# A two-layer diffusion block on Trainium2: modulation rows share the ring of raw weights

## The chip, the core and the metric

The kernel runs on one core of a Trainium2 chip. The core has TensorE (PE, with its weight loads as PEld), VectorE (DVE), ScalarE (ACT), GpSimd (POOL), and SyncE (SP), which here only issues DMAs. Each engine works through its own instructions in order; semaphores hold an instruction back until its inputs are there. The metric is the device time of one execution in microseconds (us), as a median of several.

## The reference

Two transformer layers work on 512 tokens `x` and 256 tokens of context, with a width of 1024, all in float32. A layer is a feed forward, an attention (grouped queries with a window in layer 0, differential in layer 1) and a second feed forward. Each is preceded by a norm with shift and gain and scaled by a gate. These nine vectors per layer are the modulation: one product of a condition with a 1024 x 9216 matrix, for the tokens and for the context.

```python
for i in range(DEPTH):
    mx = (silu_c @ ada_w[i] + ada_b[i]).reshape(B, N_MOD, 1, D)
    mc = (silu_cc @ ada_w[i] + ada_b[i]).reshape(N_MOD, D)
    fx = _swiglu(_pre(hx, norm_w[i, 0], mx[:, 0], mx[:, 1]), ffn_w_gate[i, 0], ...)
    hx = hx + 0.5 * mx[:, 2] * fx        # the same for hc with mc
    ...                                  # attention with mx[:, 3..5]
    ...                                  # second feed forward with mx[:, 6..8]
return _rmsnorm(hx, final_norm_w)
```

`_swiglu` is `(silu(h @ gate) * (h @ up)) @ down` with an inner width of 2816. In the last layer only `x` is needed behind the attention.

## The kernel before

**Tiling.** Tokens lie along the free axis (768 of them), features on the 128 partitions in 8 blocks. A float32 product is made of parts: each operand is split into a high part in the matmul's format and a low part (the rest), and three matmuls are added up: high by high, high by low, low by high.

**Weights.** `weights()` brings one unit: a DMA of 512 KB from SP into `w_raw` (L54), ACT's cast to `w_hi` (L55) and POOL's subtraction to `w_lo` (L56). All three names have two buffers each, so a unit's cast must wait until PE has finished the unit two before it. A unit of a projection serves 48 matmuls (L265).

**A feed forward** (`ffn`, run four times: in the trace from 0 to about 640 us, 1004 to 1600, 1600 to 2150 and from 2557 to the end, with the attentions between) has 22 up blocks in groups of 5, 5, 4, 4 and 4. An up block is two projections, gate and up; DVE then copies the bias columns (L270) and multiplies by the norm's `rstd` (L303), ACT makes the silu (L950), DVE the product (L952), ACT its high part `hh` (L956), POOL its low part `hl` (L957). A group's down part has eight units, one per block of the output; DVE adds each result to the residual (L310). The next group's up blocks are issued between.

**The modulation** is worked on DVE, beside the matmuls. The matrix of a layer is cut into 72 blocks of 128 output features. `ada_block` brings a block (a DMA of 512 KB from SP, L125, into one of two `ada_raw` buffers), and DVE multiplies it by the condition and sums along the row (L130, one instruction for the tokens, one for the context; from block 40 of layer 1 on for the tokens alone). `ada_open` brings the two conditions to all partitions (`s_bc`, L119) and takes their silu. The first 16 blocks of layer 0 are done in `start`, the other 56 in the first feed forward, three at the end of each up block (`per`); all 72 of layer 1 in the second one, four at the end of each up block, with `ada_open` behind that feed forward's norm.

**The order.** The program is written in Python in the order of the functions, but a scheduler (the tile framework, with a model of the timeline) sets the order on each engine, and the pools' buffers set the waits. So what stands at the end of an up block in the code doesn't stand there on DVE.

Of the kernel before, what the change touches and what calls it, by code (L numbers as in the profile page):

```python
# [17 lines left out]
P = 128  # L18
# [16 lines left out]
class Net:  # L35
# [12 lines left out]
    def weights(self, src, cols=1024):  # L48
        """A packed unit of weights from DRAM, split exactly into two float32r parts."""
        nc = self.nc  # L50
        raw = self.wp.tile([P, 1024], F32, name="w_raw")
        hi = self.wp.tile([P, 1024], F32R, name="w_hi")
        lo = self.wp.tile([P, 1024], F32R, name="w_lo")
        nc.sync.dma_start(raw[:, :cols], src)  # L54
        nc.scalar.copy(out=hi[:, :cols], in_=raw[:, :cols])  # L55
        nc.gpsimd.tensor_tensor(out=lo[:, :cols], in0=raw[:, :cols], in1=hi[:, :cols].bitcast(F32),  # L56
                                op=ALU.subtract)
        return (hi.rearrange("p (k m) -> p k m", m=P), lo.rearrange("p (k m) -> p k m", m=P))

    def gemm(self, outs, wpairs, xpairs):  # L60
        """outs[c] = sum_k w_k^T x_k[c]; w and x as pairs of float32r parts."""
        nc = self.nc
        n = len(wpairs)
        for k in range(n):
            wh, wl = wpairs[k]
            xs = xpairs[k]
            for o, (xh, xl) in zip(outs, xs):
                nc.tensor.matmul(o, wh, xh, start=(k == 0), stop=False)  # L68
            for o, (xh, xl) in zip(outs, xs):
                nc.tensor.matmul(o, wh, xl, start=False, stop=False)  # L70
            for o, (xh, xl) in zip(outs, xs):
                nc.tensor.matmul(o, wl, xh, start=False, stop=(k == n - 1))  # L72

# [1 line left out]
    def setup(self):  # L75
        nc, a, ctx = self.nc, self.a, self.ctx
        self.wp = self.sb("weights", 2)
        self.cp = cp = self.sb("consts", 1)
        self.tp = self.sb("temps", 2)
        self.tq = self.sb("temps1", 1)  # L80
        self.dp = self.tc.alloc_tile_pool(name="dram", bufs=1, space=bass.MemoryType.DRAM)
        self.sp = self.sb("smalls", 4)
        self.ident = cp.tile([P, P], F32, name="ident")
        make_identity(nc, self.ident)
        self.ones = cp.tile([P, P], F32, name="ones")
        nc.vector.memset(self.ones, 1.0)
        self.eps = cp.tile([P, 1], F32, name="eps")
        nc.vector.memset(self.eps, EPS)
        self.cos = cp.tile([P, SEQ], F32, name="cos")
        self.sin = cp.tile([P, SEQ], F32, name="sin")  # L90
        self.ada_b = cp.tile([P, 2, 72], F32, name="ada_b")
        self.norm_w = cp.tile([P, 2, 3, ND], F32, name="norm_w")
        self.final_w = cp.tile([P, ND], F32, name="final_w")
        self.mod = cp.tile([P, 2, 2, 72], F32, name="mod")
        self.rstd = cp.tile([P, T], F32, name="rstd")
        self.acc = cp.tile([P, T], F32, name="acc")
# [17 lines left out]
    def ada_open(self, pool):  # L114
        """silu of the two conditions, on every partition."""
# [6 lines left out]
    def ada_block(self, pool, l, b, engines=("vector", "vector"), q=None):  # L122
        nc = self.nc
        raw = pool.tile([P, D], F32, name="ada_raw")
# [19 lines left out]
    def ada_fix(self, l, b):  # L144
        """Bias of one block of a shift or a scale; a scale becomes the norm's gain."""
# [20 lines left out]
    def x_bias(self, l, n, xonly=False):  # L166
        """The shift vectors as two more columns."""
# [9 lines left out]
    def ssq(self, d, ps):  # L177
        """Sum of squares of block d of the residual, added up in PSUM."""
# [7 lines left out]
    def x_parts(self, l, n, d, xonly=False):  # L186
        """Block d of the residual times the norm's gain, in two parts."""
# [8 lines left out]
    def x_block(self, l, n, d, xonly=False):  # L196
        """Squares of block d of the residual, and its gained parts."""
# [12 lines left out]
    def rsqrt(self, out, ps, mean, view=None):  # L210
        """out = (ps * mean + EPS) ** -0.5 with a Newton step."""
# [15 lines left out]
    def norm(self, xonly=False, ps=None):  # L227
        """rstd of every token, on every partition."""
# [22 lines left out]
    def project(self, src, xonly=False):  # L251
        """PSUM [P, 2, n] of w^T x over all tokens (or those of x) and the bias columns."""
        ps = self.pbig.tile([P, 2, 512], F32, name="big")
        self.project_k([(self.weights(src), ps)], range(ND), xonly)
        return self.projected(ps, xonly)
# [17 lines left out]
    def project_halves(self, src, xonly=False, pool=None, tag="half"):  # L273
        """As project, one bank after the other."""
# [24 lines left out]
    def scaled(self, ps, tag, xonly=False):  # L299
        """tile [P, T]: ps * rstd."""  # L300
# [13 lines left out]
    def rope(self, u, bias, out, sin_engine=None):  # L314
        """out = rotated (u + bias) over the tokens of x; u is overwritten."""
# [13 lines left out]
    def gqa(self, after):  # L329
# [7 lines left out]
        od = self.dp.tile([4, 2, P, 2, T], F32, name="god")     # by group: parts of the outputs  # L337
# [26 lines left out]
        def do_q(i, pool=None):  # L364
            """Two heads; the parts of each stacked, in either order."""
# [12 lines left out]
        def do_k(i, early=None):  # L378
            """Two groups; each part twice. The keys of the context stand between the halves of x."""
# [28 lines left out]
        # per block of queries: first and number of its columns of keys, which blocks of tokens they  # L408
        # are, which mask goes where
# [9 lines left out]
        def scores(g, kk, qs, qb):  # L419
            """Softmax over keys, queries on partitions, for the four heads of a group."""  # L420
# [45 lines left out]
        def values(g, pp, qb):  # L466
            blocks = XB[qb][2]
            av = pav.tile([P, 512], F32, name="av")
            for j, b in enumerate(blocks):
                tr = ptr.tile([P, 512], F32, name="tr")  # L470
                for h in range(4):
                    # even heads first
# [8 lines left out]
            # rows 0-63 times the high parts of v, 64-127 the low ones; odd heads end in rows 64-127  # L481
# [20 lines left out]
        def out_proj(pr, os_, units, after=None):  # L502
            """Blocks of the output, the first group's part of all of them first."""
# [25 lines left out]
        # the projections that go with a step of the attention  # L529
# [46 lines left out]
    def diff(self, after):  # L576
# [15 lines left out]
        # the context's part of the residual isn't needed any more  # L592
# [18 lines left out]
        def keys(h, early=None):  # L611
# [4 lines left out]
            # parts of the first keys over each other, of the second ones the other way round  # L616
# [9 lines left out]
        def queries(h, pool=None):  # L626
# [3 lines left out]
            # each part twice  # L630
# [57 lines left out]
        def values(h, ps_, vh, vl):  # L688
# [12 lines left out]
            # norm over the head's values  # L701
# [22 lines left out]
        def out_proj(pr, os_, units, pool, tag, after=None):  # L724
            """Blocks of the output from half of the heads, the last of these behind the others."""
# [18 lines left out]
        for h in range(8):  # L744
            fill = ((), ("k",), ("q",), ("v",))
            if h == 7:
                # the normed input isn't needed any more
# [36 lines left out]
    def start(self, pool):  # L784
        """The first units of the first layer, block by block of the input as it comes."""
# [16 lines left out]
        for d in range(ND):  # L802
# [7 lines left out]
            if d < 3:  # L810
                hi, lo, src, _ = units[d]
                raw = self.wp.tile([P, 1024], F32, name="w_raw")
# [28 lines left out]
    def run(self):  # L841
# [9 lines left out]
        def to_gqa(d):  # L851
            if d == 0:
# [7 lines left out]
        self.adap = self.sb("ada1", 2)  # L860
        self.ffn(0, 1, False, [(1, b) for b in range(72)],
                 lambda d: (self.x_bias(1, 0) if d == 0 else None, self.x_block(1, 0, d)))
        self.adap.release()
        self.ffn(1, 0, False, [], lambda d: (self.x_bias(1, 1) if d == 0 else None, self.x_block(1, 1, d)))
# [4 lines left out]
        self.sp.release(); self.tq.release(); self.tp.release(); self.cp.release(); self.wp.release()  # L869
        self.dp.release()  # L870

    def finish_weights(self, d):
# [3 lines left out]
        raw = self.wp.tile([P, 1024], F32, name="w_raw")[:, :n * P]  # L876
# [6 lines left out]
    def finish(self, ws, hs):  # L883
        """The last group of the last layer and the final norm, half of the tokens after the other."""
# [35 lines left out]
    def ffn(self, l, f, xonly, side, after, first=False):  # L920
# [7 lines left out]
        per = -(-len(todo) // (NFF - 1))  # L928
# [7 lines left out]
        if side and not first:  # L936
            self.ada_open(self.adap)
# [6 lines left out]
        def up_block(i):  # L944
            pg, bg = proj(0, i)
            pu, bu = proj(1, i)
            g = self.scaled(pg, "ta", xonly)
# [11 lines left out]
            for _ in range(per):  # L959
                if todo:  # L960
                    self.ada_block(self.adap, *todo.pop(0))
            return hh, hl

        def down(g, hs, last):
# [3 lines left out]
            for d in range(ND):  # L968
# [6 lines left out]
                self.residual(outs, cuts, l, 2 if f == 0 else 8, d)  # L975
                if last:
                    after(d)
# [49 lines left out]
def _cols(w):  # L1027
    """[K, M] as units per 128 columns: [M / 128, 128, (K / 128) * 128]."""
# [4 lines left out]
def _rows4(w):  # L1033
    """[1024, 1024] as units of four row blocks and two column blocks."""
# [3 lines left out]
def _down(w):  # L1038
    """[DFF, D]: per group of row blocks and column block, row blocks side by side."""
# [8 lines left out]
def _pvec(v):  # L1048
    """[..., n * 128] with the last axis on partitions: [128, ..., n]."""
# [45 lines left out]
```

## Time and profile before

| | us |
|---|---|
| runs | 2943.73, 2944.67, 2953.78 |
| median | 2944.67 |
| span of the profiled execution | 2950.6 |
| its own time, beside the span | not listed apart from the runs |
| TensorE busy | 2792.7 |
| VectorE busy | 1562.3 |
| GpSimd busy | 1303.5 |
| ScalarE busy | 969.9 |

In the groups of a profile, a row has the line, the engine, the operation, output<-inputs by the program's names, shapes and the count; then busy time and the mean of one in ns; then the idle time of the engine just before these instructions and what ended most of it. Rows of the timeline have start, duration, engine, line and operation, and in brackets the idle time before and its releaser. In the page's slices the span is cut in 40 (73.8 us each) and a digit is the busy share in tenths.

### The profile page before, as it was taken

The numbers are of one execution on the slowest core, as the hardware profiler recorded it, in microseconds if no ns is written. First come the engines' busy times: TensorE is split into PE (matmuls) and PEld (weight loads), VectorE is DVE, ScalarE is ACT, GpSimd is POOL, SyncE is SP. The second block draws the span as 40 slices with busy tenths as digits, with TensorE's granted clock in tenths as the row PEclk, the third lists the DMA queues.
The fourth block names the chain that finished last, engine by engine and source line by source line (L and its number), as shares of the span: only waits on it lengthen the run. The fifth ranks groups of instructions, "written<-read, shape, count | busy, mean of one in ns | idle before, by whom it ended". The sixth has DMA issues, their size and how long they took to land. (4 is left out here: it accounts for less than half of the span.)

```text
span 2950.6 us, 40979 instructions
## 1 busy us (share of the span) xinstructions
PE 2792.7 (95%) x16150; PEld 2608.6 (88%) x16150; DVE 1562.3 (53%) x2683; ACT 969.9 (33%) x1749; POOL 1303.5 (44%) x762
## 2 busy tenths in 40 slices
PE   5889999999989989999999999999999999999998
PEld 4878899999878888889999999999988888799998
DVE  7999422257787799632224322223267687522223
ACT  4211122144666421112223212122245565423223
POOL 5333333354543433333335333333365665656553
PEclk8999999999999999999999999999999999999999
DMA  6355212233342445631222121221122333233331
GB/s 236 123 175 201 86 58 72 65 102 102 84 140 76 139 158 192 236 94 54 68 65 65 59 63 58 71 63 50 61 85 79 88 88 105 93 93 102 101 100 64
DMA packets 113424, 296.38 MB, mean 100 GB/s; under 512 B 12880, under 2 KB 30928, under 8 KB 113232
## 3 DMA queue, kind: packets, MB, share of 16 engines
q1 hardware_dynamic: 112944, 293.66, 31.3%
q8 instruction: 128, 2.10, 0.3%
q14 instruction: 64, 0.52, 0.1%
q10 hardware_dynamic: 288, 0.10, 0.0%
HBM read 260.42 MB, written 15.20 MB: 93 GB/s over the span
## 5 line engine op out<-in xcount | busy, mean ns | idle before, releaser
L56 POOL TENSOR_TENSOR w_lo<-w_raw,w_hi 128x1024 fp32r<-128x1024 f32 (+2 forms) x377 | 793.2, 2105 | 1057.9 <-ACT w_hi L55 1037.0
L265 PE MATMUL big<-xh,w_hi 128*128 128x384 f32 (+3 forms) x2816 | 700.7, 330 | 44.0 <-DVE xh L830 16.3
L265 PE MATMUL big<-xh,w_lo 128*128 128x384 f32 (+3 forms) x2816 | 698.9, 330 | 21.4 <-POOL w_lo L56 21.4
L265 PE MATMUL big<-xl,w_hi 128*128 128x384 f32 (+3 forms) x2816 | 696.3, 328 | 4.3 <-DVE xl L831 4.3
L55 ACT CAST w_hi<-w_raw 128x1024 fp32r<-128x1024 f32 (+2 forms) x377 | 337.1, 894 | 1100.0 <-PE big L70 340.9
L265 PEld LDWEIGHTS big<-xh,w_hi 128*128 128x128 f32 x2816 | 505.4, 192 | 54.7 <-DVE xh L830 19.6
L265 PEld LDWEIGHTS big<-xh,w_lo 128*128 128x128 f32 x2816 | 501.8, 192 | 25.1 <-POOL w_lo L56 24.8
L265 PEld LDWEIGHTS big<-xl,w_hi 128*128 128x128 f32 x2816 | 504.0, 192 | 4.8 <-DVE xl L831 4.6
L270 DVE COPY bias<-big 128x2 f32<-128x2 f32 x176 | 27.7, 157 | 743.2 <-PE big L265 743.2
L130 DVE SCALAR_TENSOR_TENSOR ada_junk<-ada_raw,s_bc 128x1024 f32<-128x1024 f32 x224 | 339.7, 1549 | 44.8 <-DMA ada_raw<-ada_w 44.0
L310 DVE SCALAR_TENSOR_TENSOR hT<-big,mod,hT 128x512 f32<-128x512 f32 (+1 forms) x288 | 168.0, 619 | 352.7 <-PE big L72 352.6
L72 PE MATMUL big<-hh,w_lo 128*128 128x512 f32 (+1 forms) x1200 | 330.0, 347 | 7.7 <-POOL w_lo L56 7.7
L68 PE MATMUL big<-hh,w_hi 128*128 128x512 f32 (+1 forms) x1200 | 329.7, 346 | 0.7 <-ACT w_hi L55 0.7
L70 PE MATMUL big<-hl,w_hi 128*128 128x512 f32 (+1 forms) x1200 | 328.0, 344 | 0.0
L957 POOL TENSOR_TENSOR hl<-tb,hh 128x768 fp32r<-128x768 f32 (+1 forms) x88 | 153.1, 1740 | 262.5 <-ACT hh L956 239.7
L72 PEld LDWEIGHTS big<-hh,w_lo 128*128 128x128 f32 x1200 | 225.5, 189 | 38.5 <-POOL w_lo L56 10.0
L70 PEld LDWEIGHTS big<-hl,w_hi 128*128 128x128 f32 x1200 | 226.8, 189 | 30.6
L68 PEld LDWEIGHTS big<-hh,w_hi 128*128 128x128 f32 x1200 | 226.2, 189 | 29.5 <-ACT w_hi L55 1.4
L956 ACT CAST hh<-tb 128x768 fp32r<-128x768 f32 (+1 forms) x88 | 68.7, 781 | 347.6 <-DVE tb L952 347.6
L284 PE MATMUL half<-xh,w_hi 128*128 128x384 f32 (+3 forms) x464 | 156.1, 336 | 21.5 <-DVE ta L296 19.7
L952 DVE SCALAR_TENSOR_TENSOR tb<-tb,bias,ta 128x512 f32<-128x512 f32 (+1 forms) x154 | 169.2, 1132 | 6.8
L284 PE MATMUL half<-xl,w_hi 128*128 128x384 f32 (+3 forms) x464 | 154.2, 332 | 0.0
(215 smaller groups left out, 3689.8 us busy)
## 6 DMA issues: line engine op xcount, KB each, us to landing
w_raw<-ffn_gu SPq DMA_DIRECT2D x176, 512.0 KB, 3.3
ada_raw<-ada_w SPq DMA_DIRECT2D x144, 512.0 KB, 3.6
w_raw<-ffn_d SPq DMA_DIRECT2D x96, 256.0 KB, 2.7
w_raw<-ffn_d SPq DMA_DIRECT2D x64, 320.0 KB, 2.9
w_raw<-diff_in SPq DMA_DIRECT2D x24, 512.0 KB, 3.3
w_raw<-gqa_in SPq DMA_DIRECT2D x12, 512.0 KB, 3.4
og<-god SPq DMA_DIRECT2D x6, 768.0 KB, 5.9
w_raw<-gqa_out SPq DMA_DIRECT2D x8, 512.0 KB, 3.6
```

The costliest lines, as they stand in the source:

```text
L55: nc.scalar.copy(out=hi[:, :cols], in_=raw[:, :cols])
L56: nc.gpsimd.tensor_tensor(out=lo[:, :cols], in0=raw[:, :cols], in1=hi[:, :cols].bitcast(F32), op=ALU.subtract)
L68: nc.tensor.matmul(o, wh, xh, start=(k == 0), stop=False)
L70: nc.tensor.matmul(o, wh, xl, start=False, stop=False)
L72: nc.tensor.matmul(o, wl, xh, start=False, stop=(k == n - 1))
L130: getattr(nc, engines[s]).scalar_tensor_tensor(out=junk, in0=raw, scalar=1.0, in1=self.sbc[:, s], op0=ALU.mult, op1=ALU.mult, accum_out=se ...
L265: mm(ps[:, c, :e - s], w[:, k], x[:, k, s:e], start=first, stop=last)
L284: mm(ps[:, :e - s], w_[:, k], x[:, k, s:e], start=(k == 0 and i == 0), stop=(k == ND - 1 and i == 2))
L310: self.nc.vector.scalar_tensor_tensor(out=h, in0=o, scalar=self.mv(l, s, c, d), in1=h, op0=ALU.mult, op1=ALU.add)
L952: nc.vector.scalar_tensor_tensor(out=u[:, tk], in0=u[:, tk], scalar=bu[:, s:s + 1], in1=g[:, tk], op0=ALU.add, op1=ALU.mult)
L956: nc.scalar.copy(out=hh[:, toks], in_=u[:, toks])
L957: nc.gpsimd.tensor_tensor(out=hl[:, toks], in0=u[:, toks], in1=hh[:, toks].bitcast(F32), op=ALU.subtract)
```

## The change

The raw blocks of the modulation take their buffers from the ring of the weights' raw units. `weights()`, `start` and `finish_weights` take `w_raw` from a new pool `raws` with four buffers, and `ada_block` takes its block from it too, in place of `ada_raw`; `w_hi` and `w_lo` keep two. In the feed forward, blocks are issued one at a time by `more()`: one between the gate and the up projection, a second behind the up projection if more than 40 blocks are on the list (the first feed forward alone, with 56), and one behind the down units 2, 4 and 6 of each group. Layer 1's blocks are halved: 36 in the second feed forward, 36 in the third. `ada_open` for layer 1 moves ahead of the second feed forward, its pool has one buffer in place of two and is released behind the third. The program is built with a smaller scratch for dynamic DMAs, which makes room. Comments and docstrings are dropped; behind the change a line's number is one higher up to the feed forward (L130 becomes L131, L265 L266, L303 L304), and nine higher in it (L952 becomes L961).

```diff
@@ weights, start, finish_weights @@
-        raw = self.wp.tile([P, 1024], F32, name="w_raw")
+        raw = self.rawp.tile([P, 1024], F32, name="w_raw")
@@ setup @@
         self.wp = self.sb("weights", 2)
+        self.rawp = self.sb("raws", 4)
@@ ada_block @@
-        raw = pool.tile([P, D], F32, name="ada_raw")
+        raw = self.rawp.tile([P, 1024], F32, name="w_raw")
@@ run @@
-        self.adap = self.sb("ada1", 2)
-        self.ffn(0, 1, False, [(1, b) for b in range(72)],
+        self.adap = self.sb("ada1", 1)
+        self.ada_open(self.adap)
+        self.ffn(0, 1, False, [(1, b) for b in range(36)],
                  lambda d: (self.x_bias(1, 0) if d == 0 else None, self.x_block(1, 0, d)))
-        self.adap.release()
-        self.ffn(1, 0, False, [], lambda d: (self.x_bias(1, 1) if d == 0 else None, self.x_block(1, 1, d)))
+        self.ffn(1, 0, False, [(1, b) for b in range(36, 72)],
+                 lambda d: (self.x_bias(1, 1) if d == 0 else None, self.x_block(1, 1, d)))
+        self.adap.release()
@@ ffn @@
         todo = list(side)
-        per = -(-len(todo) // (NFF - 1))
+
+        def more(n=1):
+            for _ in range(n):
+                if todo:
+                    self.ada_block(self.adap, *todo.pop(0))
...
         self.norm(xonly, ssq)
-        if side and not first:
-            self.ada_open(self.adap)
...
             pg, bg = proj(0, i)
+            more()
             pu, bu = proj(1, i)
+            if len(side) > 40:
+                more()
...
-            for _ in range(per):
-                if todo:
-                    self.ada_block(self.adap, *todo.pop(0))
             return hh, hl
...
                 self.residual(outs, cuts, l, 2 if f == 0 else 8, d)
+                if d in (2, 4, 6):
+                    more()
@@ kernel @@
-    nc = bacc.Bacc("TRN2", target_bir_lowering=False, num_devices=1)
+    nc = bacc.Bacc("TRN2", target_bir_lowering=False, num_devices=1, dynamic_dma_scratch_size=1024)
```

How it moves instructions is seen in the order on the engines. On DVE, in the first feed forward, this stood between the bias copies of two projections before (`ada_junk` is the product that nobody reads, `mod` gets the sums, `bias`, `ta` and `tb` belong to the projections):

```order
L270 COPY bias_846<-big_791 128x2
L303 TENSOR_TENSOR ta_905<-big_791,rstd_87 128x768
L130 SCALAR_TENSOR_TENSOR ada_junk_925,mod_86<-ada_raw_923,s_bc_102 128x1024
L130 SCALAR_TENSOR_TENSOR ada_junk_927,mod_86<-ada_raw_923,s_bc_102 128x1024
L130 SCALAR_TENSOR_TENSOR ada_junk_931,mod_86<-ada_raw_929,s_bc_102 128x1024
L130 SCALAR_TENSOR_TENSOR ada_junk_933,mod_86<-ada_raw_929,s_bc_102 128x1024
L130 SCALAR_TENSOR_TENSOR ada_junk_1063,mod_86<-ada_raw_1061,s_bc_102 128x1024
L130 SCALAR_TENSOR_TENSOR ada_junk_1065,mod_86<-ada_raw_1061,s_bc_102 128x1024
L270 COPY bias_903<-big_848 128x2
```

And this stands there now, for a whole up block:

```order
L271 COPY bias_827<-big_772 128x2
L304 TENSOR_TENSOR ta_902<-big_772,rstd_90 128x768
L131 SCALAR_TENSOR_TENSOR ada_junk_1111,mod_89<-w_raw_1109,s_bc_105 128x1024
L131 SCALAR_TENSOR_TENSOR ada_junk_1113,mod_89<-w_raw_1109,s_bc_105 128x1024
L271 COPY bias_890<-big_835 128x2
L304 TENSOR_TENSOR tb_904<-big_835,rstd_90 128x768
L131 SCALAR_TENSOR_TENSOR ada_junk_1174,mod_89<-w_raw_1172,s_bc_105 128x1024
L131 SCALAR_TENSOR_TENSOR ada_junk_1176,mod_89<-w_raw_1172,s_bc_105 128x1024
L961 SCALAR_TENSOR_TENSOR tb_904<-tb_904,bias_890,ta_902 128x256
L961 SCALAR_TENSOR_TENSOR tb_904<-tb_904,bias_890,ta_902 128x512
```

Six modulation instructions stood between two projections; now two do, behind each of them, and the second pair stands ahead of the product that `hh` is made from.

On DVE at the start of the second feed forward, where the norm's `rstd` is made (L218 to L222 before), this stood:

```order
L218 TENSOR_SCALAR tb_9129<-big_9125 128x768
L130 SCALAR_TENSOR_TENSOR ada_junk_9321,mod_86<-ada_raw_9319,s_bc_9136 128x1024
L130 SCALAR_TENSOR_TENSOR ada_junk_9323,mod_86<-ada_raw_9319,s_bc_9136 128x1024
L220 TENSOR_TENSOR tb_9129<-tb_9129,ta_9128 128x768
L130 SCALAR_TENSOR_TENSOR ada_junk_9327,mod_86<-ada_raw_9325,s_bc_9136 128x1024
L130 SCALAR_TENSOR_TENSOR ada_junk_9329,mod_86<-ada_raw_9325,s_bc_9136 128x1024
L221 SCALAR_TENSOR_TENSOR tb_9129<-tb_9129,ta_9128 128x768
```

And this now:

```order
L219 TENSOR_SCALAR tb_9137<-big_9133 128x768
L221 TENSOR_TENSOR tb_9137<-tb_9137,ta_9136 128x768
L222 SCALAR_TENSOR_TENSOR tb_9137<-tb_9137,ta_9136 128x768
L223 SCALAR_TENSOR_TENSOR rstd_90<-tb_9137,ta_9136 128x768
L131 SCALAR_TENSOR_TENSOR ada_junk_9489,mod_89<-w_raw_9487,s_bc_9012 128x1024
L304 TENSOR_TENSOR ta_9154<-big_9023,rstd_90 128x768
```

The norm's four steps have come together, with the modulation behind them.

On SP, at the same place, the queue of DMAs before (`ffn_gu` is a projection's weights, `ada_w` a modulation block):

```order
L54 DMA w_raw_9182<-ffn_gu 128x1024
L119 DMA s_bc_9136<-cond 128x1024 x2
L125 DMA ada_raw_9157<-ada_w 128x1024
L125 DMA ada_raw_9163<-ada_w 128x1024
L54 DMA w_raw_9239<-ffn_gu 128x1024
L125 DMA ada_raw_9169<-ada_w 128x1024
L125 DMA ada_raw_9175<-ada_w 128x1024
L54 DMA w_raw_9334<-ffn_gu 128x1024
```

And now, with the attention's last loads (`god`, `og3`) at its head:

```order
L120 DMA s_bc_9012<-cond 128x1024 x2
L493 DMA god_4980<-oh_8668 256x1x128
L494 DMA god_4980<-o1_8662 256x1x128
L500 DMA og3_8686<-god_4980 128x2x256 x2
L126 DMA w_raw_9146<-ada_w 128x1024
L54 DMA w_raw_9167<-ffn_gu 128x1024
L126 DMA w_raw_9223<-ada_w 128x1024
L54 DMA w_raw_9230<-ffn_gu 128x1024
L54 DMA w_raw_9299<-ffn_gu 128x1024
L126 DMA w_raw_9355<-ada_w 128x1024
L54 DMA w_raw_9362<-ffn_gu 128x1024
```

Two blocks or more went between two units of weights; now one block goes between one or two units. The conditions' DMAs (`s_bc`) stand ahead of the attention's last stores and loads.

More of the change, by code (lines that the diff above doesn't have):

```diff
@@ L811, in start @@
                 hi, lo, src, _ = units[d]
-                raw = self.wp.tile([P, 1024], F32, name="w_raw")
+                raw = self.rawp.tile([P, 1024], F32, name="w_raw")
                 nc.sync.dma_start(raw, src)
@@ L868, in run @@
         self.hp.release()
-        self.sp.release(); self.tq.release(); self.tp.release(); self.cp.release(); self.wp.release()
+        self.sp.release(); self.tq.release(); self.tp.release(); self.cp.release(); self.rawp.release(); self.wp.release()
         self.dp.release()
@@ L875, in finish_weights @@
         c = (sum(GROUPS[:-1]) * ND + d * n) * P
-        raw = self.wp.tile([P, 1024], F32, name="w_raw")[:, :n * P]
+        raw = self.rawp.tile([P, 1024], F32, name="w_raw")[:, :n * P]
         w = [self.fin.tile([P, n * P], F32R, name=f"{t}{d}") for t in ("fh", "fl")]
```

## The prediction

> **What bounds the kernel now.** First the page's busy shares and slices.
>
> ```profile
> span 2950.6 us, 40979 instructions
> PE 2792.7 (95%) x16150; PEld 2608.6 (88%) x16150; DVE 1562.3 (53%) x2683; ACT 969.9 (33%) x1749; POOL 1303.5 (44%) x762
> ...
> DVE  7999422257787799632224322223267687522223
> ```
>
> PE is busy for 95% of the span. DVE has half the work, but two stretches at 9 tenths: slices 1 to 3 counted from 0 (the first feed forward, with layer 0's modulation) and 14 to 15 (the second, with all of layer 1's). A mean hides that, so the windows come next; their columns are the stretch, its length, each engine's busy time and instructions (PE first, DVE third), the granted clock, the DMA share and GB/s.
>
> ```profile
> 110.00:340.00 230.00, 210.16 (x1118) 199.14 (x1118) 207.79 (x304) 41.83 (x56) 86.90 (x39) 0.93 0.50 165
> 340.00:640.00 300.00, 300.00 (x1708) 285.93 (x1708) 84.60 (x125) 66.91 (x90) 109.56 (x61) 1.00 0.21 65
> 1040.00:1310.00 270.00, 245.93 (x1313) 231.95 (x1312) 210.29 (x310) 50.56 (x67) 97.88 (x44) 0.94 0.53 176
> 1310.00:1600.00 290.00, 290.00 (x1650) 277.11 (x1649) 89.75 (x127) 70.89 (x97) 113.05 (x61) 1.00 0.20 62
> 1600.00:2150.00 550.00, 550.00 (x3124) 527.37 (x3123) 165.59 (x227) 129.88 (x171) 208.42 (x108) 1.00 0.20 63
> ```
>
> Without modulation PE does 1708 matmuls in 300 us, 5.693 per us, and never stops; the last two rows give 5.69 and 5.68. At this pace the 1118 of 110 to 340 need 196.4 us, so that stretch loses **33.6 us**, and the 1313 of 1040 to 1310 need 230.6, a loss of **39.4**. Both have DVE at 90% and 78% and the clock below 1. What PE waits for there (total, times, longest):
>
> ```profile
> PE big L265 <- POOL w_lo L56: 10.9, 4, 3.3
> PE big L265 <- ACT w_hi L55: 4.7, 3, 3.0
> PE big L72 <- POOL w_lo L56: 3.8, 3, 3.0
> PE big L68 <- ACT w_hi L55: 0.4, 1, 0.4
> ...
> PE big L265 <- POOL w_lo L56: 10.0, 4, 3.5
> PE big L265 <- DVE ta L303: 8.5, 1, 8.5
> PE big L72 <- POOL w_lo L56: 3.8, 3, 2.8
> PE big L265 <- ACT w_hi L55: 1.2, 2, 0.9
> PE big L68 <- ACT w_hi L55: 0.4, 1, 0.4
> ```
>
> That is 19.8 and 23.9 us of waits; the other 13.8 and 15.5 us of the losses are matmuls at the lower clock. Weights are late, but POOL and ACT are a third busy. The timeline of one such wait shows who is late:
>
> ```profile
> 150.64 0.83 ACT L956 CAST hh<-tb 128x768 fp32r<-128x768 f32 x1 [11.60 <-DVE tb L952]
> 151.38 1.04 ACT L55 CAST w_hi<-w_raw 128x1024 fp32r<-128x1024 f32 x1
> ...
> 153.38 3.33 POOL L56 TENSOR_TENSOR w_lo<-w_raw,w_hi 128x1024 fp32r<-128x1024 f32 x1
> ...
> 156.76 1.01 PE L265 MATMUL big<-xh,w_lo 128*128 128x384 f32 x2 [3.32 <-POOL w_lo L56]
> ```
>
> ACT stood 11.60 us before `hh`, for DVE, with the next weights' cast queued behind; POOL follows ACT, PE follows POOL. DVE's own account per up block (two projections):
>
> ```profile
> L130 DVE SCALAR_TENSOR_TENSOR ada_junk<-ada_raw,s_bc 128x1024 f32<-128x1024 f32 x224 | 339.7, 1549 | 44.8 <-DMA ada_raw<-ada_w 44.0
> L303 DVE TENSOR_TENSOR tb<-big,rstd 128x768 f32<-128x768 f32 x66 | 62.5, 947 | 0.0
> L952 DVE SCALAR_TENSOR_TENSOR tb<-tb,bias,ta 128x256 f32<-128x256 f32 x66 | 99.5, 1508 | 4.6
> L952 DVE SCALAR_TENSOR_TENSOR tb<-tb,bias,ta 128x512 f32<-128x512 f32 x88 | 74.7, 849 | 2.2
> L270 DVE COPY bias<-big 128x2 f32<-128x2 f32 x176 | 27.7, 157 | 743.2 <-PE big L265 743.2
> ```
>
> Its own work is 2 x 0.157 + 2 x 0.947 + 1.508 + 0.849 = 4.57 us. An up block is 96 matmuls, 96 / 5.693 = 16.86 us of PE. The order of before puts up to ten L130 between two gate copies: 10 x 1.549 + 4.57 = 20.1, more than PE needs.
>
> **The change part by part.** *Spreading.* After it the order has four L130 per up block in the first feed forward (4 x 1.549 + 4.57 = 10.8 us, 64% of 16.86) and two in the next two (7.7 us, 46%). Nothing is removed: 224 L130 before and after, 40 of them in the third feed forward, whose row above has DVE at 166 of 550 us; 40 x 1.549 = 62 makes 228. Two L130 now stand inside an up block, ahead of `hh`. What covers them, in a block without modulation:
>
> ```profile
> 404.16 0.16 DVE L270 COPY bias<-big 128x2 f32<-128x2 f32 x1 [7.45 <-PE big L265]
> ...
> 412.60 1.05 ACT L55 CAST w_hi<-w_raw 128x1024 fp32r<-128x1024 f32 x1 [3.42 <-PE big L265]
> 413.72 2.40 POOL L56 TENSOR_TENSOR w_lo<-w_raw,w_hi 128x1024 fp32r<-128x1024 f32 x1 [2.62 <-ACT w_hi L55]
> ...
> 421.10 0.16 DVE L270 COPY bias<-big 128x2 f32<-128x2 f32 x1 [7.45 <-PE big L265]
> ```
>
> The cast at 412.60 fills the slot that PE has just left, for the unit that begins at about 421.1; its low part is done at 416.12, 5.0 us early, and ACT had 3.42 us to spare ahead of the cast. Two L130 are 3.1 us, so `hh` comes 3.1 us later and neither reserve is used up; two of the longest that the trace has (3.4, a row below) are 6.8, which eats ACT's 3.42 and leaves the low part 1.6 us early. With the cover gone, each up block would lose 3.1 us, 68 in the 22 of a feed forward. I take 0, between 0 and the 29 us of the first rival. The 73.0 us of losses go, then; next late would be PE itself.
>
> *The norm at the start of the second feed forward* had L130 between its steps: the chain ran from
>
> ```profile
> 1031.06 0.94 DVE L218 TENSOR_SCALAR tb<-big 128x768 f32<-128x768 f32 x1
> ...
> 1048.96 0.95 DVE L303 TENSOR_TENSOR ta<-big,rstd 128x768 f32<-128x768 f32 x1
> ```
>
> The steps now stand together. This is the 8.5 us wait already counted in 73.0.
>
> *The shared ring.* A weight's DMA may now stand on SP behind an ada block's, which waits for DVE to read an older block; behind it queue all later weights, and ACT, POOL and PE wait for those. A late load costs its landing, cast and subtraction:
>
> ```profile
> w_raw<-ffn_gu SPq DMA_DIRECT2D x176, 512.0 KB, 3.3
> ...
> L56 POOL TENSOR_TENSOR w_lo<-w_raw,w_hi 128x1024 fp32r<-128x1024 f32 x225 | 563.6, 2505 | 699.5 <-ACT w_hi L55 689.2 <-DMA w_raw<-ffn_gu 7.5 <-ACT p L449 2.7
> ```
>
> 3.3 + 1.04 + 2.5 = 6.8 us. In the new order the read that such a load waits for stands 4 to 10 units, mostly 5 to 7, ahead of the unit that it is for (a projection's unit is 8.4 us of PE), except in the first seven units, where it is 0 to 3. I price the start at 2 us, between -6.8 (the third start unit's weights now find a free slot) and +6.8; elsewhere 0.
>
> *The opening of layer 1's modulation* moves ahead of the second feed forward: two DMAs and two Silu, now ahead of the attention's last loads on SP.
>
> ```profile
> s_bc<-cond SPq DMA_DIRECT2D x4, 512.0 KB, 5.6
> ```
>
> Two in a row, if nothing overlapped, are 11.2 us. A gain can't exceed what PE stands idle at this handover, 40.00 - 37.46 = 2.5 us:
>
> ```profile
> 1000.00:1040.00 40.00, 37.46 (x202) 36.41 (x201) 33.96 (x45) 16.42 (x18) 17.29 (x8) 0.96 0.59 197
> ```
>
> I take a loss of 2, of the size that the row has, between -2.5 and 11.2. The ring's pools, the scratch size and the text that went cost nothing on an engine; no trace here shows the scratch size, and I bound it at 0 to 2, taking 0.
>
> *Waits that stay.* A wait seen costs with its clock 33.6 / 11 = 3.1 us; I leave one or two, 4 us, between 0 and the eleven of one stage (33.6).
>
> Sum: 73.0 - 2 - 2 - 4 = **65 us**. It is made against the profiled execution: its own time isn't told beside its span, but the highest of the three runs, 2953.8, lies 3.2 above the span, and I take that one. It is 9.1 above the median, 2944.7; half of that excess, 4.5, may sit in these two stages. 2944.7 - 65 + 4.5 = **2884 us**.
>
> **Rivals.** *DVE is slowed by POOL.* The L130 of 110 to 340 lasted (min, median, max):
>
> ```profile
> L130 DVE SCALAR_TENSOR_TENSOR ada_junk<-ada_raw,s_bc x102: 1208/1218/3402, 114.5 to 314.7; 128x1024 f32<-128x1024 f32 x102
> ```
>
> The long ones lie beside a subtraction on POOL. Were all of them 3.4 in the first feed forward, a block would need 4 x 3.402 + 4.57 = 18.2 us, 1.3 over PE's, 29 us in 22 blocks: **2913 us**. Against it: POOL is busy 87 of 230 us there, and the median is 1.218. [...] By the row's mean the sum is 2884, by its maximum 2913.
>
> *Only the waits go*, and the clock stays: 13.8 + 15.5 of the gain are lost, **2913 us**. For it: the clock is 0.93 and 0.94 there. Against it: it is 1.00 in all three stretches where PE doesn't wait. [...]
>
> *The ring makes weights wait for DVE*, the other side. In the third feed forward, which lost nothing, 36 loads stand behind an ada load; if each were late by its 6.8 us, that is 245: **3129 us**. It decides where DVE reads a block only about two units ahead of need; from nine such stalls (9 x 6.8 = 61) on the kernel is slower than before. Against it: 4 to 10 units, and DVE with half of its time free.
>
> *The change doesn't spread*: the scheduler packs the blocks to the front again, **2945 us**. The order speaks against it.
>
> **How the numbers follow.** Forecast 0.76, POOL 0.10, clock 0.06, ring 0.04, no spreading 0.04. The forecast's own range: with the full 73.0, no correction and the start's gain 2944.7 - 73.0 - 6.8 = 2865; with the opening's 11.2 and two stalls more, 2884 + 9 + 14 = 2907. The two rivals at 2913 belong in the range: 2864 to 2914, which leaves out the last two and some tails, under 2 in 10. A measurement can tell about 0.5%, 14.7 us: below 2930 is faster, 0.92; within it 0.05; slower 0.03.
>
> **What would show it.** PE's waits for L55 and L56 nearly gone in the first two feed forwards, clock 1.00 and 5.69 matmuls per us there; DVE near 60% in the first, 45% in the second and 41% in the third feed forward; the norm's steps next to each other. Wrong if DVE's L130 average nearer 3.4 than 1.55, if the clock stays low without waits, if PE waits at all in the third feed forward, or if the attention's tail grows by 10 us.

## The result and the profile after

The changed kernel takes 2901.56 us (median; 2900.58 to 2902.44), the kernel before 2944.34 us, its median now over four runs. That is 42.8 us less, where 60 were forecast (2884). The ratio on record is 0.9844, 95% interval 0.9829 to 0.9859; the two medians alone give 0.9855. Two executions behind the ratios below ran in a slower state (3375.88 us of before at a granted clock of 0.749, 4588.61 us of late_again at 0.609) and are left out of them. The profiled execution ends at 2900.6 us where that of before ended at 2950.6, 50.0 earlier.

The page of the changed kernel shows these lines where the prediction shows those of before:

```profile
span 2900.6 us, 40961 instructions
PE 2770.0 (95%) x16150; PEld 2593.4 (89%) x16150; DVE 1555.9 (54%) x2683; ACT 972.4 (34%) x1749; POOL 1311.2 (45%) x762
...
DVE  7955555567887544444447333344467678522223
```

VectorE does the same work, but the stretches at 9 tenths are gone except for slice 1, counted from 0 (73 to 145 us). The windows of the changed kernel, the two stretches that lost time before among them:

```profile
110.00:340.00 230.00, 230.00 (x1311) 219.69 (x1310) 133.68 (x198) 48.10 (x63) 94.21 (x44) 1.00 0.36 119
...
960.00:1000.00 40.00, 31.80 (x167) 29.11 (x167) 33.75 (x40) 15.79 (x23) 22.84 (x11) 0.87 0.28 93
...
1040.00:1310.00 270.00, 270.00 (x1537) 259.67 (x1536) 115.97 (x168) 56.37 (x71) 103.59 (x49) 1.00 0.29 91
...
1560.00:1600.00 40.00, 38.33 (x204) 37.29 (x205) 24.17 (x34) 12.80 (x16) 13.28 (x6) 0.93 0.31 106
1600.00:1850.00 250.00, 250.00 (x1423) 239.67 (x1422) 87.56 (x124) 51.95 (x66) 94.66 (x46) 1.00 0.30 96
```

The first and third rows are what was forecast: 1311 matmuls where 1118 were, 1537 where 1313 were, 5.70 and 5.69 per us, at full clock. The second and fourth are losses at the starts of the second and third feed forward. TensorE's waits (total, times, longest) in 110 to 600, then in 930 to 1000 (the longest alone) and in 1400 to 1640:

```profile
PE big L266 <- POOL w_lo L56: 1.8, 1, 1.8
...
PE big L266 <- DVE hT L311: 8.2, 1, 8.2
...
PE big L266 <- DVE xl L194: 3.3, 1, 3.3
PE big L266 <- ACT xh L193: 2.5, 1, 2.5
```

The eleven weight waits of the first feed forward have become one. What TensorE waits for now is the input of the next feed forward: the residual (`hT`) and its parts (`xh`, `xl`). Ahead of the second feed forward the wait for `hT` was 2.5 us before and is 8.2 now; the third one had no wait at its start before.

How the modulation is paced shows in the groups of the changed kernel:

```profile
L131 DVE SCALAR_TENSOR_TENSOR ada_junk<-w_raw,s_bc 128x1024 f32<-128x1024 f32 x224 | 342.4, 1546 | 291.6 <-DMA w_raw<-ada_w 290.4
```

The mean is as before (1546 against 1549 ns). But VectorE now stands 290 us before these instructions, for their loads, where it was 44 us: the blocks come at the pace of their loads.

To see where the rest of the 73 us went, the span is cut at places that both programs have in the same order on TensorE. Each cut is the start of the last instruction of a group: the matmuls of the start's sum of squares, the last L72 of a feed forward, the output projection's last matmul, the first matmul of the last feed forward's norm. The view of one line, for L72 in the second feed forward, of before and after (duration min/median/max, first and last start; the last start is the cut):

```profile
L72 PE MATMUL big<-hh,w_lo x102: 278/338/398, 1500.5 to 1604.1; 128*128 128x256 f32 x51, 128*128 128x512 f32 x51
```

```profile
L72 PE MATMUL big<-hh,w_lo x128: 277/337/401, 1430.4 to 1547.3; 128*128 128x256 f32 x64, 128*128 128x512 f32 x64
```

The stretches between cuts in us, for all profiles; a stretch's name is what it ends with, and each feed forward's start counts to it:

| kernel | start | feed forward 1 | attention 1 | feed forward 2 | feed forward 3 | attention 2 | rest | span |
|---|---|---|---|---|---|---|---|---|
| before | 42.9 | 614.2 | 344.7 | 602.3 | 559.0 | 407.5 | 380.0 | 2950.6 |
| before_again | 41.4 | 611.5 | 343.9 | 598.6 | 558.8 | 407.7 | 380.1 | 2942.0 |
| after | 47.5 | 581.2 | 349.5 | 569.1 | 567.3 | 405.9 | 380.1 | 2900.6 |
| after_again | 46.8 | 581.9 | 349.3 | 569.3 | 568.0 | 407.3 | 380.1 | 2902.7 |
| two_rings | 43.3 | 611.1 | 354.7 | 607.5 | 558.8 | 406.1 | 380.1 | 2961.6 |
| ring_alone | 44.8 | 602.2 | 345.6 | 584.6 | 558.6 | 405.6 | 380.2 | 2921.6 |
| late_blocks | 46.6 | 582.0 | 351.8 | 560.5 | 558.8 | 405.4 | 380.1 | 2885.2 |
| late_again | 44.5 | 584.3 | 346.9 | 562.7 | 559.0 | 406.2 | 380.2 | 2883.8 |
| late_open_late | 46.0 | 583.3 | 349.5 | 563.5 | 558.6 | 406.4 | 380.4 | 2887.7 |
| all72 | 46.4 | 581.7 | 348.9 | 587.9 | 558.9 | 405.8 | 380.2 | 2909.8 |
| start_third_later | 41.3 | 584.4 | 348.3 | 569.3 | 568.5 | 407.2 | 380.1 | 2899.1 |
| all_three | 41.4 | 585.0 | 345.9 | 562.5 | 558.9 | 406.4 | 380.1 | 2880.2 |

Before to after: the first two feed forwards give 33.0 and 33.2, the second attention 1.6; the start takes 4.6, the attention 4.8, the third feed forward 8.3. That is 50.1, and 50.0 by the spans.

### The profile page after: what moved, and what is told of

The parts are those of the page before. It is cut to its first block, busy times and chain, and to the rows that moved or that the text cites. A ratio compares the mean times of both kernels' runs of the same rounds, so it can differ in the third digit from the quotient of the medians.

```text
span 2900.6 us, 40961 instructions
## 1 busy us (share of the span) xinstructions
PE 2770.0 (95%) x16150; PEld 2593.4 (89%) x16150; DVE 1555.9 (54%) x2683; ACT 972.4 (34%) x1749; POOL 1311.2 (45%) x762
## 5 line engine op out<-in xcount | busy, mean ns | idle before, releaser
L56 POOL TENSOR_TENSOR w_lo<-w_raw,w_hi 128x1024 fp32r<-128x1024 f32 (+2 forms) x377 | 802.1, 2128 | 1072.1 <-ACT w_hi L55 1055.6
L266 PE MATMUL big<-xh,w_hi 128*128 128x384 f32 (+3 forms) x2816 | 696.6, 328 | 38.7 <-DVE xh L831 19.5
L266 PE MATMUL big<-xl,w_hi 128*128 128x384 f32 (+3 forms) x2816 | 693.6, 327 | 8.3 <-DVE xl L832 5.0
L266 PE MATMUL big<-xh,w_lo 128*128 128x384 f32 (+3 forms) x2816 | 693.6, 328 | 2.3 <-POOL w_lo L56 2.3
L266 PEld LDWEIGHTS big<-xh,w_hi 128*128 128x128 f32 x2816 | 502.5, 191 | 47.2 <-DVE xh L831 22.3
L266 PEld LDWEIGHTS big<-xl,w_hi 128*128 128x128 f32 x2816 | 500.3, 191 | 10.5 <-DVE xl L832 6.3
L266 PEld LDWEIGHTS big<-xh,w_lo 128*128 128x128 f32 x2816 | 497.8, 190 | 3.8 <-POOL w_lo L56 3.3
L131 DVE SCALAR_TENSOR_TENSOR ada_junk<-w_raw,s_bc 128x1024 f32<-128x1024 f32 x224 | 342.4, 1546 | 291.6 <-DMA w_raw<-ada_w 290.4
L72 PE MATMUL big<-hh,w_lo 128*128 128x512 f32 (+1 forms) x1200 | 326.8, 344 | 0.0
L70 PEld LDWEIGHTS big<-hl,w_hi 128*128 128x128 f32 x1200 | 226.1, 188 | 29.5
L72 PEld LDWEIGHTS big<-hh,w_lo 128*128 128x128 f32 x1200 | 225.0, 188 | 28.6
L961 DVE SCALAR_TENSOR_TENSOR tb<-tb,bias,ta 128x512 f32<-128x512 f32 (+1 forms) x154 | 176.1, 1177 | 8.7 <-DVE tb L304 0.5
L285 PE MATMUL half<-xh,w_hi 128*128 128x384 f32 (+3 forms) x464 | 155.5, 335 | 20.6 <-DVE ta L297 18.8
```

The costliest lines, as they stand in the source:

```text
L131: getattr(nc, engines[s]).scalar_tensor_tensor(out=junk, in0=raw, scalar=1.0, in1=self.sbc[:, s], op0=ALU.mult, op1=ALU.mult, accum_out=se ...
L266: mm(ps[:, c, :e - s], w[:, k], x[:, k, s:e], start=first, stop=last)
L285: mm(ps[:, :e - s], w_[:, k], x[:, k, s:e], start=(k == 0 and i == 0), stop=(k == ND - 1 and i == 2))
L961: nc.vector.scalar_tensor_tensor(out=u[:, tk], in0=u[:, tk], scalar=bu[:, s:s + 1], in1=g[:, tk], op0=ALU.add, op1=ALU.mult)
```

## The experiments

**before_again.** The kernel before, unedited.

> The kernel before, profiled once more. The changed kernel's trace ends 50.0 us earlier than that of before (2900.6 against 2950.6), but its median only 42.8 us earlier. Theory P: the profiled execution of before was about 9 us longer than a usual one; then this span is 2941 to 2944, and the missing 6 to 9 us lie in the two packed stretches (last L72 of the first feed forward before 657.1, from the first to the last matmul of the second one under 599.4 us). Rival: the span is 2949 to 2952 again, and it is the changed kernel whose trace flatters it.

The span is 2942.0, its time 2943.81, so theory P holds: the first profile of before was 8.6 us long. The table puts 1.5 of it in the start, 2.7 in the first and 3.7 in the second feed forward. The stretches with waits differ between these two executions; the third feed forward, which has none, differs by 0.2.

**two_rings.** The new placement, with a ring of two for each kind:

```diff
-        self.rawp = self.sb("raws", 4)
+        self.rawp = self.sb("raws", 2)
+        self.adar = self.sb("ada_raws", 2)
@@ ada_block @@
-        raw = self.rawp.tile([P, 1024], F32, name="w_raw")
+        raw = self.adar.tile([P, 1024], F32, name="ada_raw")
```

> The new placement (one block behind the gate projection, one behind every second down unit, halves for layer 1) with two buffers for weights and two for modulation blocks, as before. Theory S (the shared ring does the spreading, since a block's load must wait its turn among the weights): the order on VectorE has 6, 4, 6, 4 modulation instructions between two bias copies again, as before, and the time is that of before, 2935 to 2946. Rival C (the placement in the code spreads, the ring only saves room): 2895 to 2906, as the changed kernel.

Ratio 1.0043 (1.0027 to 1.0059): rival C falls. Theory S is right about the order and wrong about the time, which is above its 2946. In the first feed forward the new places in the code do nothing by themselves: on VectorE the numbers of modulation instructions between two bias copies are those of before, copy for copy (6 1 1 0 3 3 6 6 4 6 5 5 and so on), and the stretch takes 611.1 us where before_again takes 611.5. The windows of this kernel, and its waits in 980 to 1310, show the late weights of before again, and a longer wait for the residual:

```profile
110.00:340.00 230.00, 210.86 (x1133) 199.87 (x1132) 205.81 (x304) 41.77 (x56) 87.44 (x39) 0.95 0.50 170
1040.00:1310.00 270.00, 249.91 (x1353) 237.23 (x1352) 211.66 (x298) 55.53 (x71) 98.57 (x44) 0.96 0.50 170
```

```profile
PE big L267 <- DVE hT L312: 15.3, 1, 15.3
PE big L267 <- POOL w_lo L56: 11.3, 5, 3.3
PE half L521 <- DMA og<-god: 5.3, 1, 5.3
```

With the conditions opened early, 14 modulation instructions of the second feed forward start ahead of its first matmul, where before had none, 11 of them in the attention's tail. The wait ahead of the second feed forward is 15.3 us, and the attention takes 10.8 more than in before_again; that these instructions cost the attention its time is argued, not shown.

**ring_alone.** The ring of four, everything else placed as before. Beside the lines shown, the opening stands behind the second feed forward's norm again, and the third has no blocks:

```diff
             pg, bg = proj(0, i)
-            more()
             pu, bu = proj(1, i)
-            if len(side) > 40:
-                more()
...
+            more(-(-len(side) // (NFF - 1)))
             return hh, hl
...
-                if d in (2, 4, 6):
-                    more()
...
-        self.ffn(0, 1, False, [(1, b) for b in range(36)],
+        self.ffn(0, 1, False, [(1, b) for b in range(72)],
```

> The shared ring of four with the old placement: three or four blocks at the end of each up block, all 72 of layer 1 in the second feed forward, the conditions opened behind its norm. Theory S: the ring alone holds the blocks back, if in lumps (0 to 10 instructions between two bias copies, 4 on average): most of the gain, 2900 to 2920, with some waits for w_lo left. Rival C: 2940 to 2946.

Ratio 0.9928 (0.9912 to 0.9943), some 2923 us by the first chip's 2944. It is less than half of the change's gain (0.7% of 1.6%), so theory S's "most of the gain" fails, and the time is just outside what it gave. The ring holds the blocks back, but in lumps, and nine short waits of a projection for `w_lo` are left in 110 to 660 where the changed kernel has one of 1.8 us:

```profile
PE big L266 <- POOL w_lo L56: 10.1, 9, 2.6
```

The modulation instructions also last longer here, 1776 ns in the mean where the changed kernel has 1546. So both parts are needed: the ring to bind the blocks to the weights, the placement to set at which weight. The first feed forward shows it best, since neither the halving nor the opening of layer 1 touches it: of 611.5 us in before_again the places alone save 0.4, the ring alone 9.3, both together some 30 (581.2 and 581.9).

**late_blocks.** In the second and third feed forward the first block comes with up block 4:

```diff
             pg, bg = proj(0, i)
-            more()
+            if first or i >= 4:
+                more()
             pu, bu = proj(1, i)
-            if len(side) > 40:
+            if first or i in (6, 9, 12, 15):
                 more()
```

> The changed kernel, but in the second and third feed forward the first block is issued behind up block 4, and up blocks 6, 9, 12 and 15 have a second one. Theory H (the next feed forward's first blocks are pulled forward among the residual's and the norm's inputs on VectorE at the two handovers): TensorE's wait ahead of the second feed forward falls from 8.2 to about 2.5 us, the waits of 3.3 and 2.5 us ahead of the third one go, with the clock 0.93 there: 8.6 and 8.3 us of loss go, 2883 to 2890. Rival O (the early opening's two DMAs and Silu delay the attention's tail): only the third feed forward's part goes, 2892 to 2896. Rival R (neither): 2899 to 2904.

Ratio 0.979 (0.9767 to 0.9812). The third feed forward is at 558.8, as before the change, so its whole loss was these blocks. The second is 8.6 shorter, and the wait ahead of it fell from 8.2 to 1.6 (930 to 1060):

```profile
PE big L266 <- DVE hT L311: 1.6, 1, 1.6
```

Over all profiles this wait goes with the number of modulation instructions that start ahead of the second feed forward's first matmul: it is 1.6 to 3.1 us with none (before, and all kernels with late blocks), 8.2 to 8.7 with four (the changed kernel and start_third_later), 13.1 with six (all72), 12.9 with seven (ring_alone) and 15.3 with 14 (two_rings). At the other handover, VectorE's timeline in the changed kernel, where the second feed forward's last down group feeds the third:

```profile
1541.75 1.13 DVE L311 SCALAR_TENSOR_TENSOR hT<-big,mod,hT 128x256 f32<-128x256 f32 x2
1542.81 1.27 DVE L131 SCALAR_TENSOR_TENSOR ada_junk<-w_raw,s_bc 128x1024 f32<-128x1024 f32 x1
...
1544.01 2.07 DVE L194 SCALAR_TENSOR_TENSOR xl<-hT,mod,xh 128x256 fp32r<-128x256 f32 x1
1546.00 3.42 DVE L131 SCALAR_TENSOR_TENSOR ada_junk<-w_raw,s_bc 128x1024 f32<-128x1024 f32 x1
...
1549.34 0.74 DVE L194 SCALAR_TENSOR_TENSOR xl<-hT,mod,xh 128x512 fp32r<-128x512 f32 x1
1550.01 1.13 DVE L311 SCALAR_TENSOR_TENSOR hT<-big,mod,hT 128x256 f32<-128x256 f32 x2
1551.06 0.48 DVE L194 SCALAR_TENSOR_TENSOR xl<-hT,mod,xh 128x256 fp32r<-128x256 f32 x1
1553.15 1.94 DVE L131 SCALAR_TENSOR_TENSOR ada_junk<-w_raw,s_bc 128x1024 f32<-128x1024 f32 x1 [1.60 <-DMA w_raw<-ada_w]
```

These L131 belong to the third feed forward's first up blocks: the second one's 72 have all run by 1523. One of them even waits 1.60 us for its load, with the residual queued behind. In late_blocks the same place reads:

```profile
1535.06 1.13 DVE L311 SCALAR_TENSOR_TENSOR hT<-big,mod,hT 128x256 f32<-128x256 f32 x2
1536.11 0.48 DVE L194 SCALAR_TENSOR_TENSOR xl<-hT,mod,xh 128x256 fp32r<-128x256 f32 x1
1537.78 1.84 DVE L194 SCALAR_TENSOR_TENSOR xl<-hT,mod,xh 128x512 fp32r<-128x512 f32 x1 [1.18 <-ACT xh L193]
1539.54 1.13 DVE L311 SCALAR_TENSOR_TENSOR hT<-big,mod,hT 128x256 f32<-128x256 f32 x2
```

A block of the residual takes 4.5 us here (1535.06 to 1539.54), and 8.3 there (1541.75 to 1550.01). The attention's stretch did not get shorter, 351.8.

**late_open_late.** As late_blocks, with `ada_open` behind the norm:

```diff
         self.adap = self.sb("ada1", 1)
-        self.ada_open(self.adap)
...
         self.norm(xonly, ssq)
+        if side and l == 0 and not first:
+            self.ada_open(self.adap)
```

> As late_blocks, and the conditions of layer 1 are opened behind the second feed forward's norm again. Theory O2 (the two DMAs of the conditions, ahead of the last stores and loads on SP, cost the attention's tail time of its own: from the first feed forward's last L72 to the output projection's last matmul it took 351.8 us in late_blocks, 343.9 in the second profile of before): this stretch is 343 to 346 us, and the ratio to before falls from 0.979 to 0.976 to 0.977. Rival: the tail's loss is the blocks' own loads and stays at 349 to 352, ratio 0.979.

Theory O2 falls: the attention takes 349.5, the ratio is 0.9794 (0.978 to 0.9809), and what the attention lost by 2.3 less the second feed forward took, by 3.0 more. With the early opening the same stretch takes 351.8 and 346.9 in two profiles of one kernel (late_blocks and late_again, below), so this doesn't show that the opening makes the tail longer. It doesn't rule it out either: the three profiles with the ring of four and the late opening have 345.6, 349.5 and 345.9, those with the early one 346.9 to 351.8.

**all72.** All of layer 1 in the second feed forward:

```diff
-        self.ffn(0, 1, False, [(1, b) for b in range(36)],
+        self.ffn(0, 1, False, [(1, b) for b in range(72)],
...
-        self.ffn(1, 0, False, [(1, b) for b in range(36, 72)],
+        self.ffn(1, 0, False, [],
...
-                if d in (2, 4, 6):
+                if d in ((1, 2, 3, 4, 5, 6, 7) if len(side) > 60 else (2, 4, 6)):
                     more()
```

> The changed kernel, but all 72 blocks of layer 1 in the second feed forward (two per up block, the rest behind seven of eight down units), none in the third. Theory: four instructions per up block hide there as they do in the first feed forward, so the second one is no longer than in the changed kernel (569 us from output projection's last matmul to its own last L72), and the third loses its 8.5 us of handover: 2890 to 2895, ratio 0.981 to 0.983. Rival: the halving is needed, waits for w_lo come back in the second feed forward, 2905 to 2925, ratio 0.986 to 0.992.

Ratio 0.987 (0.9848 to 0.9892): the rival holds. The third feed forward gets its 8.4 us back, but the second takes 18.8 more. Its waits in 977 to 1300:

```profile
PE big L266 <- DVE hT L311: 13.1, 1, 13.1
PE big L266 <- POOL w_lo L56: 2.5, 2, 2.0
PE big L266 <- ACT w_hi L55: 2.4, 1, 2.4
PE big L72 <- POOL w_lo L56: 1.8, 2, 1.1
```

More of the blocks are pulled into the handover (six instructions against four, a wait of 13.1 against 8.2), and the weights are late again here and there. So halving is worth 10.4 us even with its own handover loss in it.

**start_third_later.** The third start unit's load comes two input blocks later in the code:

```diff
-            if d < 3:
-                hi, lo, src, _ = units[d]
+            if d in (0, 1, 4):
+                hi, lo, src, _ = units[min(d, 2)]
```

> The changed kernel, with the third start unit's load issued two input blocks later in the code. Theory: its DMA at 15.09 us, which stands ahead of the input's last blocks, is what makes the start 4 to 6 us longer; the sum of squares ends at 41 to 44 us instead of 47.5 and the first feed forward's last L72 at 623 to 626 instead of 628.7. Rival: the start is longer because of the blocks' loads further on; 627 to 631.

One execution, 2900.84 us. The start is at 41.3 again, from 47.5, so the load makes the start longer: SP's queue of the changed kernel has it ahead of the input's last blocks,

```profile
15.09 0.33 SPq L814 DMA_DIRECT2D w_raw<-ffn_gu  x1
16.37 1.60 SPq L798 DMA_DIRECT2D hT<-xT  x2
```

and before, the third unit's load went out at 24.86, behind the input's last blocks. But the first feed forward takes 3.2 more: its last L72 is at 625.7, 3.0 earlier than in the changed kernel. Half of the start's loss was a shift. The other profiles bear this out: in the six whose start and first feed forward are those of the changed kernel, the start took 44.5 to 47.5 us, but the last L72 of the first feed forward lay at 628.1 to 629.3.

**all_three.** Late blocks, late opening and the later third unit in one.

> Late blocks, late opening and the later third start unit together. If the three losses are separate and each is what it was taken for, the span is that of the changed kernel less 8.5 (third feed forward), 6 (handover to the second), 6 (attention's tail) and 4 (start): 2876, ratio 0.975 to 0.977. If the parts overlap, 0.978 to 0.980.

Ratio 0.9791 (0.9777 to 0.9806), as for late_blocks alone: the median doesn't tell the two apart, and the parts don't add up to the 24.5 us expected. The span, 2880.2, is 20.4 below the changed kernel's, but its execution (2882.03) was the shortest of four, 5.4 under their median.

**after_again and late_again.** The changed kernel and late_blocks side by side.

> The changed kernel again, on the same chip as the next run, for two questions: what a stretch that no edit touches differs by from one profile of the same kernel to the next, and what the late blocks are worth side by side. If the attention's stretch (349.5 us in the first profile, 343.9 and 344.7 in those of before) comes out at 348 to 351, its loss belongs to the change; at 344 to 347 it is the spread of profiles. Ratio 0.984 to 0.985.

> late_blocks again. Theory H: below the changed kernel by 8.5 us in the third feed forward and by 6 to 9 in the second, ratio 0.978 to 0.980, with intervals apart from the changed kernel's; the waits ahead of the second and third feed forward's first projections below 2.5 us in total each. Rival (the gain of late_blocks was its chip's): ratio 0.982 to 0.985.

The changed kernel is at 0.9844 (0.9821 to 0.9867), late_blocks at 0.9783 (0.9761 to 0.9806), with the intervals apart: 2903.95 and 2885.62 us on one chip. The changed kernel's stretches repeat within 1.4 us each, its attention within 0.2 (349.3), so by the expectation those 5 us belong to the change. But late_blocks repeats its attention only within 5 (351.8 and 346.9), so two profiles that agree are weak evidence. The rest of theory H holds in late_again: the second feed forward is 6.6 below that of after_again and the third 9.0, and the waits ahead of them are 2.3 us and none.

## Why the prediction was right in the range and 18 us off

**What bounds the kernel** was right. VectorE's lump held `hh`, the casts and the weights back, and with the lump went the waits (19.8 us in 110 to 340 before, none now) and the low clock (0.93 before, 1.00 now): 33.0 of 33.6 us in the first feed forward. In the second, 38.9 of 39.4 came back from its first matmul on (599.4 us to 560.5); its wait for the residual, 5.7 longer than before, left 33.2. Against the second profile of before the two feed forwards gain less, 30.3 and 29.5. VectorE's busy share came as foretold: 58% and 43% in the two windows above, and 41% in the third feed forward (235.50 of 568 us from 1547 to 2115).

**Spreading: right in its effect, without its cause.** The prediction read the even order off the changed kernel and saw the ring as a risk alone. two_rings shows that the places without the ring give the old order in the first feed forward, and ring_alone that the ring without the places gives less than half. What spreads is the two together: with the ring a block's load stands between two units' loads and waits its turn, seen in VectorE's 290 us before L131, and the place in the code sets between which units.

**Terms of the sum that were mis-sized**, against the first profile of before:
- *The opening and the tail*, priced at 2 between -2.5 and 11.2: 5.7 us of longer wait ahead of the second feed forward and 4.8 us in the attention, 10.5. That is near the upper end, but the end was made of two DMAs in a row. The longer wait was another thing, the next feed forward's blocks pulled in among the residual's steps (late_blocks); what the 4.8 are is not shown.
- *Waits that stay*, priced at 4 as late weights: such waits of a projection came to 2.3 us in all. Instead the third feed forward lost 8.3 us at its start, which stands in the sum at nothing. This is the step that failed: "What covers them" was answered for an up block, where VectorE has a reserve, and not for the last down group, where each residual block is on the way to TensorE's next matmul. The prediction's own signs caught it: "if PE waits at all in the third feed forward" came true, with 5.8 us at its start, and "if the attention's tail grows by 10 us" nearly so, if the wait behind it is counted.
- *The start*, priced at 2: 4.6 against one profile, 6.1 against the other. The price's sign was right; its reason (weights that wait for VectorE) wasn't the one found. The third unit, from which a gain was thought possible, got its buffer early and took the input's turn. With 3.0 of it real, by the last L72, the price was near.
- *The profiled execution's excess*: half of 9.1 was taken, with the execution guessed to be that of 2953.8. Wherever the runs list both, an execution's time is 1.7 to 2.2 us above its span, never 3.2, so the profiled one took about 2952.4, an estimate, 8.1 above the median of 2944.34. The second profile of before has 8.6 of its span gone, 7.9 in the start and the first two feed forwards. 7.2 (50.0 - 42.8) is missing from the median's gain: the 8.1, less the 0.9 by which the changed kernel's profiled execution was above its own median.

Together: 73.0 - 1.1 - 10.5 - 8.3 - 4.6 + 1.6 = 50.1 in place of 65, and 7.2 in place of 4.5 for the excess. (The 1.1 is what the two feed forwards fell short of 73.0; the 1.6 is in the second attention, where two profiles of the changed kernel differ by 1.4.) The range held the result because its upper part was built of two DMAs, of stalls and of rivals that didn't come. That it was wide enough for the handovers too is luck.

**The rivals.** POOL did not slow VectorE more: L131's mean is 1546 ns, where L130's was 1549. The clock came back as the waits went: 1.00 in both stretches, where it was 0.93 and 0.94, and 0.93 and 0.87 where the waits are now. In 110 to 340 us of the kernel before, the mean clock was 0.93 with no wait above 3.3 us; how long a wait must be to lower the clock, no run shows. The ring did not make weights wait for VectorE: in 1000 to 1400 and in 1640 to 2000 TensorE never waits.

**What stays open** is the attention's 5 us. They repeat in the changed kernel, and late_blocks had them once and half of them the other time. The modulation instructions in its tail don't explain them, since late_blocks has none there and took 351.8. Whether the early opening has a part in them isn't settled.

## What to carry to other kernels

A shared ring is a way to pace side work: what must take a buffer between two weights didn't run ahead of them here (VectorE stood 290 us before its blocks' loads, where it was 44), while a place in the code alone held nothing (611.1 us for the first feed forward against 611.5), where the scheduler pulled the work forward. The ring needed the even places to go with it (0.9928 alone, 0.9844 with them). Look at the handovers separately: the same engine that has half of its time free inside a stage (VectorE, busy for 43% of 1040 to 1310) can be the one that is waited for where the stage's last results become the next one's input (8.2 us ahead of the second feed forward, 5.8 ahead of the third). Here the side work's first pieces were pulled in just there. Four up blocks' delay was worth 0.6% more (0.9844 to 0.9783), and that version beats both kernels.

## What was not expected of the hardware

Two profiles of one kernel differed by 8.6 us in 2945 where it has waits, and by 0.2 in a stretch of 559 us that has none. In the changed kernel, most of whose waits are gone, two profiles differ by 2.1. That the waits are the reason isn't shown: late_blocks has fewer still, and its attention differs by 4.9. A comparison of single profiles is only as good as the repeatability of the stretches compared.
